# Seven block products in three PSUM banks, six such pairs a layer, in an encoder kernel on one core

## The chip, the core and the metric

The kernel runs on one core of a Trainium2 chip. TensorE (PE) multiplies matrices into PSUM, eight banks of 512 float32 columns for each of the 128 partitions; VectorE (DVE), ScalarE (ACT) and GpSimd (POOL) work on SBUF and PSUM; SyncE (SP) issues transfers. Each engine runs its own instructions in the order in which the program gives them, and waits on semaphores for the others. The metric is the device time of one execution in microseconds.

## The reference

Two layers over x of 512 positions and 1024 channels, in float32. Cut to what matters here:

```python
h = rmsnorm(x, norm1[l])
p = h @ w_in[l]                                # Fourier group | q | k | v
y_f = fourier_mix(u, w_fourier[l], b_fourier[l])
y_a = windowed_gqa(q, k, v, sink[l])
mix = concat([rmsnorm(y_f, ...), rmsnorm(y_a, ...)])
x = x + mix @ w_o[l]
h = rmsnorm(x, norm2[l])
up = dwconv_centred(h @ w_up[l], conv_w[l], conv_b[l])
gate, val = up[..., :D_FF], up[..., D_FF:]     # D_FF = 2816
x = x + (silu(gate) * val) @ w_down[l]
```

The convolution has width 3 along the positions. The change lies in the last four lines, the ConvFFN.

## The kernel before

Channels lie on partitions, positions along the free dimension, so `x` is eight tiles of 128x512. A float32 product is made of three matmuls of rounded parts (`mm3`: high by high on L121, low by high on L122, high by low on L123). A weight tile is split by `wsplit` into `whi` (ACT, L91) and `wlo` (DVE, L94: the raw tile less its high part); there are five buffers of each. Raw weights (`wraw`, three buffers) come by SP (L130).

The FFN of a layer goes over 22 pairs `fi` of channel blocks (gate and value), in groups of 8, 7 and 7 pairs; after each group its part of `w_down` is multiplied, eight output blocks of 8 or 7 blocks deep. A pair is made in one of two ways:

- `up_eight`: for gate and value each, two splits and 24 matmuls of 512 columns into one bank, then one DVE multiplication by `rb2` (the reciprocal norm, by position) out of PSUM.
- `up_seven`: gate and value are taken together as a 2 by 2 block product, over two halves of the input channels and two halves of the positions (`LO` and `HI`, 256 columns), with seven block products in place of eight (the Winograd form). That is 84 matmuls of 256 columns. The weights of four of the products are the sums s1 to s4 that DVE makes in `tA` tiles; seven tiles are split. X, Y and Z are sums in PSUM: X holds B11, then T2 is added, then T3 or T4; Y holds T1, then B22 is added; Z holds B21. Between the steps ACT copies X and Y out (`act(ua..)`, `act(ub..)`) and DVE adds. Before, X and Y are the two halves of one bank and Z is in a second.

The seven products of the activations need sums of the normed blocks too (T1 to T4); `sums_of_h` makes them once a layer: ACT loads eight blocks, DVE makes 16 subtractions or additions of 256 columns and eight low parts of 512, into `m4` tiles and the `room` tiles. T1 and T3 lie in one tile, T2 and T4 in another.

Then follow for each pair the convolution (`conv`: ACT once, DVE twice on L97, for gate and for value), silu on ACT, a product on DVE and its split into `slab` or `pT`.

Beside this, layer 0 splits part of layer 1's weights ahead (`presplit`): one job per pair or per `w_down` block loads a tile (`praw`, by SP), splits it into two `tA` tiles on ACT and DVE, and stores both to DRAM (`kept`), 88 stores in all, on SP's queue one job late (`late`, `store`). Layer 1 fetches them.

`rb2` comes from a sum of squares: transposing matmuls, DVE makes `nv` (L208), POOL raises it to the power -1/2 (`nr`, L210), PE broadcasts it (L233), ACT copies it out (`rb`). The order of the instructions on each engine comes from the framework's scheduler, which simulates the engines over the program; the program's own order is what it starts from. PSUM banks are taken in turn from the list `FFN_BANKS`, whose names stand for pools of three (`mm`), two (`sc`, `tp`) and one (`av`) banks. There are six `tF`, six `tA` and two `praw` buffers.

Of the kernel before, what the change touches and what calls it, by code (L numbers as in the profile page):

```python
# [12 lines left out]
ALU = mybir.AluOpType  # L13
# [15 lines left out]
FT = DFF // P  # L29
# [1 line left out]
NEG = -1.0e30  # L31
NWARM = 10
RATE, STEP0 = 1, 12
FFN_BANKS = ("mm", "mm", "mm", "av", "sc", "sc")
GROUPS = [(0, 8), (8, 7), (15, 7)]
SEVEN = [range(2, FT, 3), range(2, FT, 3)]


def encoder_kernel(tc, t):
# [7 lines left out]
    nc = tc.nc  # L47
# [9 lines left out]
    tp = pool(name="temps", bufs=2)  # L57
# [11 lines left out]
    def f(x):  # L69
        return x.bitcast(F32)  # L70
# [19 lines left out]
    def act(out, in_, func=AF.Copy, **kw):  # L90
        return nc.scalar.activation(out, in_, func, **kw)  # L91

    def tt(out, a, b, op, eng=None):
        return (eng or nc.vector).tensor_tensor(out, a, b, op=op)  # L94
# [41 lines left out]
    def wsplit(raw, eng=None, hi_eng=None):  # L136
        hi = wp.tile([P, 512], F32R, tag="whi", name=nm("whi"), bufs=5)
        lo = wp.tile([P, 512], F32R, tag="wlo", name=nm("wlo"), bufs=5)
        n = raw.shape[-1]
        if hi_eng is None:  # L140
            pace[0] = act(hi[:, :n], raw).ins
        else:
            hi_eng.tensor_copy(hi[:, :n], raw)
        tt(lo[:, :n], raw, f(hi)[:, :n], ALU.subtract, eng)
        return hi, lo
# [5 lines left out]
    kept = {}  # L151

    def presplit(l):

        late = []

        def keep(key, src):
            n = src.shape[-1]
            two = [temp(n, "tA", F32R) for _ in range(2)]
            with tc.issue_after(pace[0]):  # L160
                act(two[0], src)
            tt(two[1], src, f(two[0]), ALU.subtract)
            kept[key] = [dp.tile([P, n], F32, tag=f"{key}{s}", name=nm("kept")) for s in range(2)]
            store()
            late.append(lambda: [nc.sync.dma_start(o, f(z)) for o, z in zip(kept[key], two)])

        def store():
            while late:
                late.pop()()

        def load(src):
            raw = temp(512, "praw")[:, :src.shape[-1]]
            nc.sync.dma_start(raw, src)
            return raw

        jobs = []
        for grp in (1, 0):
            for k in range(KT):
                c = (k % 2) * 384
                jobs.append((f"qkv{grp}{k}", lambda g=grp, k=k, c=c: load(t["w_qkv"][l, g, k // 2, :, c:c + 384])))  # L180
        for k in range(KT):
            jobs.append((f"u{k}", lambda k=k: load(t["w_in"][l, k * P:(k + 1) * P, 0:FW])))
        for j in range(NF):
            jobs.append((f"f{j}", lambda j=j: load_wf(l, j, temp(512, "praw"))))
        for half in range(2):
            for m in range(KT):
                jobs.append((f"o{half}{m}", lambda h=half, m=m: load(t["w_o"][l, h, :, m * 512:(m + 1) * 512])))
        got = jobs[0][1]()
        for n, (key, _) in enumerate(jobs):
            raw = got  # L190
            if n + 1 < len(jobs):
                got = jobs[n + 1][1]()
            keep(key, fold_wu(raw) if key[0] == "u" else fold_wf(raw) if key[0] == "f" else raw)
            yield
        store()
        while True:
            yield

# [181 lines left out]
    LO, HI = slice(0, 256), slice(256, 512)  # L380

    def bank():
        nps[0] += 1
        return psum(FFN_BANKS[nps[0] % len(FFN_BANKS)])

# [9 lines left out]
    def sums_of_h(l, h2):  # L395

        room = rooms()
        out = []
        for k in range(4):
            b = [temp(512, "tF") for _ in range(2)]  # L400
            for i in range(2):
                act(b[i], x[k + 4 * i], scale=g2[:, l, k + 4 * i:k + 4 * i + 1])
            t13, t24 = temp(512, "tF"), temp(512, "tF")
            tt(t13[:, LO], b[0][:, HI], b[0][:, LO], ALU.subtract)
            tt(t13[:, HI], b[1][:, HI], b[0][:, HI], ALU.subtract)
            tt(t24[:, LO], t13[:, LO], b[1][:, HI], ALU.subtract)
            tt(t24[:, HI], t24[:, LO], b[1][:, LO], ALU.add)
            r13, r24 = [next(room), next(room)], [next(room), next(room)]
            split(*r13, t13)
            split(*r24, t24)  # L410
            out.append(dict(B11=[z[:, LO] for z in halves(h2[k])], B21=[z[:, LO] for z in halves(h2[k + 4])],
                            B22=[z[:, HI] for z in halves(h2[k + 4])], T1=[z[:, LO] for z in r13],
                            T3=[z[:, HI] for z in r13], T2=[z[:, LO] for z in r24], T4=[z[:, HI] for z in r24]))
        return out
# [14 lines left out]
    def up_seven(l, fi, h2, ts, rb2):  # L429
        a, b = [wload(t["w_up"][l, fi + z * FT], 1024) for z in range(2)]  # L430
        a11, a12, a21, a22 = a[:, :512], a[:, 512:], b[:, :512], b[:, 512:]
        xy, zz = bank(), bank()
        X, Y, Z = xy[:, LO], xy[:, HI], zz[:, LO]
        ua, ub = temp(512, "tF"), temp(512, "tF")

        def product(o, w, key, start=False):
            for k in range(4):
                mm3(o, [z[:, k * P:(k + 1) * P] for z in w], ts[k][key], start and k == 0, k == 3, skip_group_check=True)

        product(X, wsplit(a11), "B11", True)  # L440
        act(ua[:, LO], X)
        s1, s2, s3, s4 = [temp(512, "tA") for _ in range(4)]
        tt(s1, a21, a22, ALU.add)
        product(Y, wsplit(s1), "T1")
        act(ub[:, HI], Y)
        tt(s3, a11, a21, ALU.subtract)
        tt(s2, s3, a22, ALU.subtract)
        product(X, wsplit(s2), "T2")
        act(ua[:, HI], X)
        product(Z, wsplit(a12), "B21", True)  # L450
        tt(ua[:, LO], ua[:, LO], Z, ALU.add)
        product(X, wsplit(s3), "T3")
        tt(ub[:, HI], ub[:, HI], X, ALU.add)
        tt(s4, a12, s2, ALU.add)
        product(Y, wsplit(s4), "B22")
        tt(ua[:, HI], ua[:, HI], Y, ALU.add)
        tt(ua, ua, rb2, ALU.mult)
        yield ua
        product(X, wsplit(a22), "T4")
        tt(ub[:, LO], X, rb2[:, LO], ALU.mult)  # L460
        tt(ub[:, HI], ub[:, HI], rb2[:, HI], ALU.mult)
        yield ub
# [11 lines left out]
    for l in range(L):  # L474
# [4 lines left out]
        for grp in (1, 0):  # L479
# [14 lines left out]
            z = temp(1536, "pT").rearrange("p (b c) -> p b c", b=NB)  # L494
# [303 lines left out]
        if l == 0:  # L798
            tabs, alts, wt = load_tables(1)
        ahead = presplit(l + 1) if l < L - 1 else iter(lambda: 0, 1)  # L800
        ts = sums_of_h(l, h2)
        for f0, nf in GROUPS:
            gu = []
            for fi in range(f0, f0 + nf):
                n = fi - f0
                ys_ = [conv(l, fi + z * FT, u) for z, u in enumerate((up_seven if fi in SEVEN[l] else up_eight)(l, fi, h2, ts, rb2))]
                next(ahead)
                act(ys_[0], ys_[0], AF.Silu)
                tt(ys_[0], ys_[0], ys_[1], ALU.mult)
                if n < 4:  # L810
                    a = pair("slab")
                else:
                    if n % 2 == 0:
                        two = temp(2048, "pT", F32R).rearrange("p (n s q) -> p n s q", n=2, s=2)
                    a = two[:, n % 2]
                split(a[:, 0, :], a[:, 1, :], ys_[0])
                gu.append(a)
            nxt = []
            for m in range(KT):
                next(ahead)  # L820
                w = wchunks(t["w_down"][l, m, :, f0 * P:(f0 + nf) * P], nf * P)
                end = l == L - 1 and f0 + nf == FT
                nh = 2 if end and m == KT - 1 else 1
                for h in range(nh):
                    q0, q1 = h * S // nh, (h + 1) * S // nh
                    o = bank()[:, q0:q1]
                    for k in range(nf):
                        mm3(o, [z[:, (k % 4) * P:(k % 4 + 1) * P] for z in w[k // 4]],
                            [gu[k][:, s, q0:q1] for s in range(2)], k == 0, k == nf - 1)
                    tt(x[m][:, q0:q1], x[m][:, q0:q1], o, ALU.add)  # L830
                    if end:
                        nc.sync.dma_start(t["out"][m, :, q0:q1], x[m][:, q0:q1])
                if l < L - 1 and f0 + nf == FT:
                    nxt.append(norm_tile(m, g1[:, l + 1, :], acc))
            xg = nxt
# [88 lines left out]
```

## Time and profile before

| | |
|---|---|
| median of 2 runs | 1152.34 us (1151.12 to 1153.57) |
| profiled execution | 1152.17 us, span 1150.4 us, mean granted TensorE clock 0.966 |
| PE busy | 1064.2 us, 93% of the span |
| DVE busy | 813.5 us, 71% |
| ACT busy | 549.2 us, 48% |
| POOL busy | 65.3 us, 6% |
| FFN of layer 0 | about 201 to 581 us of the span |
| FFN of layer 1 | about 763 to 1150 us of the span |

A row of the profile names the line, the engine, the operation and its tiles without their numbers (`tF<-ps` reads PSUM and writes a tF tile). Times are microseconds from the span's start. In brackets stands the time that the engine was idle before, and what ended it. Matmuls are pipelined, so their cost is read from start to start, not from the length of one. Instructions of a helper carry the helper's line: L91 is every ACT operation, L94 every two-input DVE operation, so they are told apart by their tiles.

### The profile page before, as it was taken

How to read it: one execution, taken by the hardware profiler on the slowest of the kernel's cores; microseconds unless marked ns; L12 is line 12 of the kernel's file. 1: busy time of each engine (PE TensorE's matmuls, PEld its weight loads, DVE VectorE, ACT ScalarE, POOL GpSimd, SP SyncE). 2: the span in 40 equal slices, each digit the busy share in tenths (PEclk: the TensorE clock that was granted, in tenths of full speed). 3: DMA queues.
4: the chain of work that ended last, by engine and by line, in shares of the span. 5: the costliest groups of instructions: out<-in, count | busy, mean ns of one | idle time of the engine just before them, and what ended most of it. 6: DMA issues, size and time to landing. Idle time of an engine off the chain costs nothing.

```text
span 1150.4 us, 15741 instructions
## 1 busy us (share of the span) xinstructions
PE 1064.2 (93%) x5599; PEld 910.9 (79%) x5599; DVE 813.5 (71%) x1624; ACT 549.2 (48%) x1055; POOL 65.3 (6%) x142
## 2 busy tenths in 40 slices
PE   8998899789997989997999989996899989999898
PEld 7976688678886878787879967885788878778787
DVE  7967669786758778667676866496865487647863
ACT  5259637554434444344443595264543354324541
POOL 0005200000000000000010052020000000000000
PEclk9999999899999989988999999998999999999999
DMA  8220032334843438544677402521233222232233
GB/s 274 75 91 20 19 98 87 114 102 151 246 155 126 153 111 280 173 135 140 191 237 222 164 19 76 182 74 57 91 100 102 92 75 87 80 123 79 88 85 101
DMA packets 60547, 140.13 MB, mean 122 GB/s; under 512 B 6706, under 2 KB 20274, under 8 KB 60468
## 3 DMA queue, kind: packets, MB, share of 16 engines
q1 hardware_dynamic: 60468, 139.12, 38.1%
q8 instruction: 44, 0.72, 0.2%
q14 instruction: 35, 0.29, 0.1%
HBM read 116.02 MB, written 23.07 MB: 121 GB/s over the span
## 4 chain that ended last, share of the span: by engine, by line
PE 66%; DVE 18%; issue 8%; ACT 4%; DMA 3%; POOLq 1%; POOL 0%; SPq 0%; DVEq 0%; ACTq 0%
PE ps L121 20%; PE ps L122 20%; PE ps L123 19%; DVE tF L97 5%; DVE tF L94 3%; DVE tA L94 3%; PE ps L119 3%; DVE wlo L94 3%; DMA wraw<-in_w_up_dram 1%; PE ps L644 1%; ACT tA L91 1%; PE ps L625 1%; PE ps L637 1%; DVE tA L629 1%; DMA wraw<-in_w_qkv_dram 1%
## 5 line engine op out<-in xcount | busy, mean ns | idle before, releaser
L91 ACT ACTIVATE whi<-wraw 128x512 fp32r<-128x512 f32 (+1 forms) x282 | 169.5, 613 | 291.8 <-PE ps L123 256.5
L122 PE MATMUL ps<-act,wlo 128*128 128x512 f32 (+1 forms) x712 | 262.1, 369 | 0.4 <-DVE wlo L94 0.4
L94 DVE TENSOR_TENSOR wlo<-wraw,whi 128x512 fp32r<-128x512 f32 (+1 forms) x290 | 189.5, 664 | 102.5 <-ACT whi L91 100.4
L121 PE MATMUL ps<-act,whi 128*128 128x512 f32 (+1 forms) x712 | 260.9, 369 | 0.0
L123 PE MATMUL ps<-act,whi 128*128 128x512 f32 (+1 forms) x712 | 260.9, 368 | 0.0
L122 PEld LDWEIGHTS ps<-act,wlo 128*128 128x128 f32 x712 | 136.9, 192 | 22.5 <-DVE wlo L94 1.0
L121 PEld LDWEIGHTS ps<-act,whi 128*128 128x128 f32 x712 | 137.1, 192 | 21.4
L123 PEld LDWEIGHTS ps<-act,whi 128*128 128x128 f32 x712 | 136.8, 192 | 21.1
L97 DVE SCALAR_TENSOR_TENSOR tF<-tF,pb,tF 128x511 f32<-128x511 f32 x176 | 127.7, 743 | 4.4 <-ACT tF L91 3.6
L121 PE MATMUL ps<-slab,whi 128*128 128x512 f32 (+2 forms) x276 | 105.7, 386 | 3.1 <-ACT slab L91 2.6
L122 PE MATMUL ps<-slab,wlo 128*128 128x512 f32 (+2 forms) x276 | 105.6, 383 | 1.8 <-DVE wlo L94 1.8
L123 PE MATMUL ps<-slab,whi 128*128 128x512 f32 (+2 forms) x276 | 105.3, 384 | 1.1 <-DVE slab L94 1.1
L91 ACT ACTIVATE tF<-tF,pb 128x512 f32<-128x512 f32 x88 | 71.3, 811 | 44.9 <-DVE tF L94 23.5
L121 PE MATMUL ps<-m,whi 128*128 128x256 f32 x140 | 46.2, 330 | 47.2 <-ACT whi L91 25.3
L94 DVE TENSOR_TENSOR tF<-ps,rb 128x512 f32<-128x512 f32 (+1 forms) x90 | 57.0, 642 | 36.3 <-PE ps L123 31.8
L94 DVE TENSOR_TENSOR x<-x,ps 128x512 f32<-128x512 f32 (+1 forms) x65 | 42.6, 675 | 56.4 <-PE ps L123 56.4
L121 PEld LDWEIGHTS ps<-m,whi 128*128 128x128 f32 x140 | 31.0, 222 | 52.5 <-ACT whi L91 26.6
L121 PEld LDWEIGHTS ps<-slab,whi 128*128 128x128 f32 x276 | 52.1, 189 | 14.6 <-ACT slab L91 3.5
L122 PE MATMUL ps<-pT,wlo 128*128 128x512 f32 (+1 forms) x163 | 62.9, 387 | 0.5 <-DVE wlo L94 0.5
L121 PE MATMUL ps<-pT,whi 128*128 128x512 f32 (+1 forms) x163 | 62.9, 387 | 0.1
L122 PEld LDWEIGHTS ps<-slab,wlo 128*128 128x128 f32 x276 | 52.2, 189 | 11.9 <-DVE wlo L94 2.1
L123 PEld LDWEIGHTS ps<-slab,whi 128*128 128x128 f32 x276 | 52.1, 189 | 11.8 <-DVE slab L94 1.9
(192 smaller groups left out, 1897.1 us busy)
## 6 DMA issues: line engine op xcount, KB each, us to landing
wraw<-in_w_up_dram SPq DMA_DIRECT2D x88, 512.0 KB, 3.6
kept<-tA SPq DMA_DIRECT2D x56, 256.0 KB, 3.4
wraw<-in_w_down_dram SPq DMA_DIRECT2D x32, 448.0 KB, 3.4
wraw<-in_w_down_dram SPq DMA_DIRECT2D x16, 512.0 KB, 3.7
whi<-kept SPq DMA_DIRECT2D x28, 256.0 KB, 3.5
wlo<-kept SPq DMA_DIRECT2D x28, 256.0 KB, 3.7
kept<-tA SPq DMA_DIRECT2D x32, 192.0 KB, 2.8
wraw<-in_w_o_dram SPq DMA_DIRECT2D x8, 512.0 KB, 3.7
```

The lines of the kernel that those rows point to most:

```text
L91: return nc.scalar.activation(out, in_, func, **kw)
L94: return (eng or nc.vector).tensor_tensor(out, a, b, op=op)
L97: return nc.vector.scalar_tensor_tensor(out=out, in0=a, scalar=s, in1=b, op0=op0, op1=op1)
L119: nc.tensor.matmul(out, a[0], b[0], start=start, stop=stop, **kw)
L121: nc.tensor.matmul(out, a[0], b[0], start=start, stop=False, **kw)
L122: nc.tensor.matmul(out, a[1], b[0], start=False, stop=False, **kw)
L123: nc.tensor.matmul(out, a[0], b[1], start=False, stop=stop, **kw)
L625: nc.tensor.matmul(sc[:, :n], qT[p][:, e, i * P:(i + 1) * P], kT[g][:, s, j0 * P:(j1 + 1) * P], start=s == 0, stop=s == 1)
L629: nc.vector.tensor_tensor_reduce(out=pr[:, :n], in0=sc[:, :n], in1=mask[:, m0:m0 + n], scale=qs_scale[p][:, i, e:e + 1], scalar=nsink[:, l ...
L637: tr = nc.tensor.transpose(pp[:, j * P:(j + 1) * P], pr[:, j * P:(j + 1) * P], ident)
L644: pv = nc.tensor.matmul(py[64 * e:64 * e + 64, i0 * P:(i1 + 1) * P], vp[:, j, 64 * g:64 * g + 64], pT[:, half, e, b0:b0 + 2 * (i1 - i0) + ...
```

## The change

Five edits, all in the FFN:

- `SEVEN` begins with pair 5 in place of pair 2: pairs 5, 8, 11, 14, 17, 20 of each layer are seven pairs, and pair 2 is an eight pair.
- X, Y and Z of a seven pair get a bank each, and the products alternate between them: B11 (X), T1 (Y), B21 (Z), T2 (X), B22 (Y), T3 (X), T4 (X). Before, the program has B11, T1, T2, B21, T3, B22, T4.
- `FFN_BANKS` has the two `tp` banks as well, eight in all.
- `sums_of_h` is called after the first pair of the layer and its `presplit` job, not ahead of the loop.
- The stores of `presplit` are issued by GpSimd's queue at once, not by SP's one job later.

```diff
-FFN_BANKS = ("mm", "mm", "mm", "av", "sc", "sc")
+FFN_BANKS = ("mm", "mm", "mm", "av", "sc", "sc", "tp", "tp")
-SEVEN = [range(2, FT, 3), range(2, FT, 3)]
+SEVEN = [range(5, FT, 3), range(5, FT, 3)]
...
             kept[key] = [dp.tile([P, n], F32, tag=f"{key}{s}", name=nm("kept")) for s in range(2)]
-            store()
-            late.append(lambda: [nc.sync.dma_start(o, f(z)) for o, z in zip(kept[key], two)])
-
-        def store():
-            while late:
-                late.pop()()
+            for o, z in zip(kept[key], two):
+                nc.gpsimd.dma_start(o, f(z))
...
-        xy, zz = bank(), bank()
-        X, Y, Z = xy[:, LO], xy[:, HI], zz[:, LO]
+        X, Y, Z = [bank()[:, LO] for _ in range(3)]
...
         tt(s1, a21, a22, ALU.add)
-        product(Y, wsplit(s1), "T1")
+        product(Y, wsplit(s1), "T1", True)
         act(ub[:, HI], Y)
+        product(Z, wsplit(a12), "B21", True)
+        tt(ua[:, LO], ua[:, LO], Z, ALU.add)
         tt(s3, a11, a21, ALU.subtract)
         tt(s2, s3, a22, ALU.subtract)
         product(X, wsplit(s2), "T2")
         act(ua[:, HI], X)
-        product(Z, wsplit(a12), "B21", True)
-        tt(ua[:, LO], ua[:, LO], Z, ALU.add)
+        tt(s4, a12, s2, ALU.add)
+        product(Y, wsplit(s4), "B22")
         product(X, wsplit(s3), "T3")
         tt(ub[:, HI], ub[:, HI], X, ALU.add)
-        tt(s4, a12, s2, ALU.add)
-        product(Y, wsplit(s4), "B22")
...
-        ts = sums_of_h(l, h2)
+        ts = None
...
                 next(ahead)
+                if ts is None:
+                    ts = sums_of_h(l, h2)
```

The order in which the scheduler then puts the instructions, at three places. ACT in layer 1, around the first copy out of X in pair 11, before: `ps_1978` is the bank of X and Y, `whi_1994`, `whi_1996` and `whi_1999` are the pair's last three split weights, `slab` and the `tF` rows with `pb` are the pairs ahead of it.

```order
L91 ACTIVATE whi_1994_9154<-tA_1986_9098 128x512
L91 ACTIVATE tF_1966_9021<-tF_1965_9019,pb_96 128x512
L91 ACTIVATE whi_1996_9172<-tA_1987_9099 128x512
L91 ACTIVATE whi_1999_9194<-wraw_1977_9073 128x512
L91 ACTIVATE tF_1974_9062<-tF_1973_9060,pb_96 128x512
L91 ACTIVATE slab_1958_8981<-tF_1949_8934 128x512
L91 ACTIVATE tF_1980_9077<-ps_1978_9075 128x256
L91 ACTIVATE tF_1966_9021<-tF_1966_9021 128x512
L91 ACTIVATE tF_1981_9078<-ps_1978_9075 128x256
```

And now, with X in `ps_1966` and Y in `ps_1967`; `whi_1983`, `whi_1985` and `whi_1988` are the last three weights.

```order
L91 ACTIVATE whi_1983_9038<-tA_1976_8982 128x512
L91 ACTIVATE whi_1985_9054<-tA_1975_8981 128x512
L91 ACTIVATE slab_1946_8863<-tF_1937_8816 128x512
L91 ACTIVATE tF_1962_8944<-tF_1961_8942,pb_96 128x512
L91 ACTIVATE tF_1969_8960<-ps_1966_8957 128x256
L91 ACTIVATE whi_1988_9077<-wraw_1965_8955 128x512
L91 ACTIVATE tF_1954_8903<-tF_1954_8903 128x512
L91 ACTIVATE tF_1970_8961<-ps_1967_8958 128x256
```

The pair's last weight moved from ahead of X's copy to behind it, and the two copies read two banks.

DVE in layer 0, from `nv` to the first multiplications by `rb2` (`rb_418`), before: the 128x256 rows and the rows into `m4` and `room` belong to `sums_of_h`.

```order
L208 TENSOR_SCALAR nv_415_1884<-ps_414_1879 128x4
L94 TENSOR_TENSOR wlo_492_2135<-wraw_488_2128,whi_491_2134 128x512
L94 TENSOR_TENSOR tF_446_1961<-tF_445_1960,tF_444_1957 128x256
L94 TENSOR_TENSOR m4_442_1951<-tF_440_1945,m4_442_1951 128x512
L94 TENSOR_TENSOR wlo_509_2193<-wraw_502_2184,whi_508_2192 128x512
L94 TENSOR_TENSOR tF_446_1961<-tF_446_1961,tF_444_1957 128x256
```

And now, the same place; `wlo_504` to `wlo_514` are weights of pair 2, an eight pair.

```order
L201 TENSOR_SCALAR nv_415_1884<-ps_414_1879 128x4
L94 TENSOR_TENSOR wlo_504_2189<-wraw_502_2186,whi_503_2188 128x512
L94 TENSOR_TENSOR wlo_506_2193<-wraw_502_2186,whi_505_2192 128x512
L94 TENSOR_TENSOR wlo_512_2230<-wraw_510_2227,whi_511_2229 128x512
L94 TENSOR_TENSOR tF_437_1959<-ps_436_1934,rb_418_1893 128x512
L94 TENSOR_TENSOR wlo_514_2234<-wraw_510_2227,whi_513_2233 128x512
L94 TENSOR_TENSOR tF_445_2000<-ps_444_1975,rb_418_1893 128x512
```

The sums that stood ahead of `rb2`'s first use now follow it, among the convolutions of the first pairs.

SP at the end of layer 0's FFN, before: loads for `presplit` (`praw`) and stores (`kept`) in turn.

```order
L173 DMA praw_1221_5417<-in_w_o_dram 128x512
L165 DMA kept_1212_5375<-tA_1210_5371 128x512
L165 DMA kept_1224_5423<-tA_1222_5419 128x512
L173 DMA praw_1234_5466<-in_w_o_dram 128x512
L165 DMA kept_1225_5424<-tA_1223_5420 128x512
L130 DMA wraw_1280_5652<-in_w_down_dram 128x896
```

And now; the stores stand on POOL's queue.

```order
L130 DMA wraw_1260_5517<-in_w_down_dram 128x896
L167 DMA praw_1192_5266<-in_w_o_dram 128x512
L167 DMA praw_1204_5313<-in_w_o_dram 128x512
L130 DMA wraw_1268_5556<-in_w_down_dram 128x896
L167 DMA praw_1217_5362<-in_w_o_dram 128x512
```

SP's queue holds loads alone in this stretch.

More of the change, by code (lines that the diff above doesn't have):

```diff
@@ L153, in presplit @@
     def presplit(l):
-        late = []
         def keep(key, src):
@@ L194, in presplit @@
             yield
-        store()
         while True:
```

## The prediction

> **What bounds the kernel now.** I read the page's busy times and its chain first, then both FFN stretches side by side, then what TensorE waited for ahead of the seven products, then the single waits.
>
> ```profile
> PE 1064.2 (93%) x5599; PEld 910.9 (79%) x5599; DVE 813.5 (71%) x1624; ACT 549.2 (48%) x1055; POOL 65.3 (6%) x142
> PE 66%; DVE 18%; issue 8%; ACT 4%; DMA 3%; POOLq 1%; POOL 0%; SPq 0%; DVEq 0%; ACTq 0%
> ```
>
> TensorE (PE) is busy 93% of the span and holds two thirds of the chain. So the time can fall in two ways only: fewer matmul columns, or fewer gaps and half-clock matmuls. The stretch view (us; busy PE, PEld, DVE, ACT, POOL; granted clock; DMA share; GB/s) gives the FFN of layer 0, then that of layer 1:
>
> ```profile
> 201.00:555.00 354.00, 316.41 (x1601) 272.62 (x1600) 256.69 (x444) 160.73 (x277) 0.00 (x0) 0.94 0.49 155
> 768.00:1151.00 383.00, 355.03 (x1817) 303.80 (x1815) 257.34 (x423) 163.29 (x272) 8.28 (x1) 0.97 0.28 88
> ```
>
> PE is without work for 354.00 - 316.41 = 37.6 us in the first and 383.00 - 355.03 = 28.0 us in the second, at clocks of 0.94 and 0.97. Most of that stands ahead of the T products of the seven-product pairs. The tile view of `m` (the tiles m4 that hold most T sums) names for each window what ended PE's idle time, in us and number of times; the first three lines are layer 0, the last is layer 1:
>
> ```profile
>   ACT whi L91: 25.3, 6
>   DVE wlo L94: 11.1, 6
>   ACT tF L91: 0.5, 1
> ```
>
> ```profile
>   ACT tF L91: 21.4, 12
> ```
>
> The causes differ. In layer 0 T1 waits for its weights: s1 is made late on VectorE (DVE), so its high part (and behind it the low part) comes late. In layer 1 the weights are there, and T1 and T2 wait for ScalarE (ACT) to evict X, with which Y shares a bank. PE's timeline around single waits, with the idle time and its releaser in brackets:
>
> ```profile
> 212.66 0.58 PE L121 MATMUL ps<-m,whi 128*128 128x256 f32 x1 [6.67 <-ACT whi L91]
> 252.48 0.38 PE L121 MATMUL ps<-m,whi 128*128 128x256 f32 x1 [3.38 <-ACT whi L91]
> 370.79 0.58 PE L121 MATMUL ps<-m,whi 128*128 128x256 f32 x1 [5.26 <-ACT whi L91]
> 410.30 0.41 PE L121 MATMUL ps<-m,whi 128*128 128x256 f32 x1 [3.37 <-ACT whi L91]
> 488.57 0.38 PE L121 MATMUL ps<-m,whi 128*128 128x256 f32 x1 [2.85 <-ACT whi L91]
> 528.61 0.39 PE L121 MATMUL ps<-m,whi 128*128 128x256 f32 x1 [3.79 <-ACT whi L91]
> 778.49 0.38 PE L233 MATMUL ps<-ident,nr 128*128 128x128 f32 x1 [2.48 <-POOL nr L210]
> 793.13 0.58 PE L121 MATMUL ps<-m,whi 128*128 128x256 f32 x1 [7.18 <-ACT tF L91]
> 830.01 0.39 PE L121 MATMUL ps<-m,whi 128*128 128x256 f32 x1 [2.73 <-ACT tF L91]
> ...
> 830.54 0.41 PE L121 MATMUL ps<-m,whi 128*128 128x256 f32 x1
> ...
> 832.25 0.41 PE L123 MATMUL ps<-room,whi 128*128 128x256 f32 x1
> ```
>
> These are pairs 2, 5, 11, 14, 17 and 20 of layer 0, then rb2 and pairs 2 and 5 of layer 1. The matmuls behind a wait run slower: from 830.54 to 832.25 are eight starts, 0.214 us each.
>
> **PE's own work.** At full clock, three spacings of 512 columns lie between the first two rows, three of 256 between the last two:
>
> ```profile
> 203.72 0.39 PE L121 MATMUL ps<-act,whi 128*128 128x512 f32 x1
> ...
> 204.40 0.28 PE L121 MATMUL ps<-act,whi 128*128 128x256 f32 x1
> ...
> 204.75 0.28 PE L121 MATMUL ps<-act,whi 128*128 128x256 f32 x1
> ```
>
> 0.68 / 3 = 0.227 and 0.35 / 3 = 0.117. An eight pair is 48 x 0.227 = 10.9 us, a seven pair 84 x 0.117 = 9.8 to 10.0. Pair 2 of each layer becomes an eight: +0.9 us per layer, on the path wherever PE sets the end (in layer 1 in full).
>
> **Layer 1, the banks.** With X, Y, Z apart, T1 (in Y) needs no eviction, and its weights are early: in the new order DVE makes s1 of pair 5 ahead of the evictions of pairs 2 to 4. What comes next is T2, which goes into X and stands 24 matmuls (T1 and B21, 2 x 1.4 = 2.8 us) behind B11, where before only B21 lay between. How long ACT takes to that eviction is seen in pair 5:
>
> ```profile
> 827.37 0.63 ACT L91 ACTIVATE whi<-wraw 128x512 fp32r<-128x512 f32 x1 [0.70 <-ACT whi L91]
> 827.90 0.80 ACT L91 ACTIVATE tF<-tF,pb 128x512 f32<-128x512 f32 x1
> 829.06 0.63 ACT L91 ACTIVATE slab<-tF 128x512 fp32r<-128x512 f32 x1 [0.35 <-DVE tF L94]
> 829.59 0.37 ACT L91 ACTIVATE tF<-ps 128x256 f32<-128x256 f32 x1
> ```
>
> B21 ended at 830.01 - 2.73 = 827.28, and only then could this weight tile be overwritten; convolution, slab and eviction follow, ending 2.7 us later. In the new order of pairs 11, 14, 17 and 20 ACT's last weight split ahead of the eviction takes B11's buffer, so the same row of work starts at B11's end and is done some 2.7 us later, against T2's 2.8. That just fits; I keep 0.6 us of wait for each of five pairs. In pair 5 a split for the next pair (waiting for B21's buffer) stands ahead of the eviction, and PE has that pair's first 12 matmuls between: I keep 1.3 us (a split of 0.63 and as much again from engine to engine, as in the 0.70 before 827.37). So 21.4 - 5 x 0.6 - 1.3 = 17.1 us go. Both ends: 21.4 if nothing waits, and 21.4 - 6 x 2.73 = 5.0 if every pair waits as pair 5 does now (pair 2's own wait goes in any case, since it is no longer a seven). I take 17.1, as the rows of ACT name the work exactly.
>
> The half-clock matmuls behind those waits: about 13 a pair x (0.214 - 0.117) = 1.2 us, five long waits, 6 us; with waits under 1.3 us I let 5 go. The Trainium skill, "TensorE: Matmul & The Clock Gate", Part 1, has the clock fall after an idle window of about 3.4 us; the row at 830.54 shows slow matmuls after 2.73 us already, which that free-running window does not forbid. By the rule alone only pair 2's wait would have cost clock for certain, and the term would be 1.2 instead of 5.
>
> **Layer 1, sums_of_h later.** Its 16 half-wide and 8 full subtractions stood on DVE while POOL took the power for rb2:
>
> ```profile
> 194.99 1.39 POOL L210 TENSOR_TENSOR nr<-nv,mhalf 128x4 f32<-128x4 f32 x1 [47.31 <-DVE nv L208]
> 770.15 8.28 POOL L210 TENSOR_TENSOR nr<-nv,mhalf 128x4 f32<-128x4 f32 x1 [49.87 <-DVE nv L208]
> ```
>
> Now weight subtractions that wait for buffers follow nv, and the sums come behind rb2's first evictions. I take the power at 1.4 us, the other row, so PE's 2.48 us at 778.49 go. The Trainium skill, "SBUF — State Buffer", Who interferes with whom, says that a DVE instruction with two SBUF inputs and a GpSimd one that reads SBUF lock each other out whole; the 8.28 agrees, the 1.39 beside equally dense DVE work does not. Layer 1: -17.1 - 5 - 2.5 + 0.9 = -23.7 us.
>
> **Layer 0.** There DVE is the late one, and the sums move into its full stretch. The same stretch view for the sums' place now, and from rb2 to the wait of pair 5; below it DVE's first eviction and s1 of pair 5:
>
> ```profile
> 188.00:202.50 14.50, 14.50 (x73) 12.28 (x72) 12.85 (x29) 11.19 (x20) 1.39 (x1) 1.00 0.14 40
> 202.50:252.30 49.80, 38.09 (x201) 33.05 (x200) 39.91 (x67) 26.66 (x46) 0.00 (x0) 0.90 0.36 115
> ```
>
> ```profile
> 202.70 1.89 DVE L94 TENSOR_TENSOR tF<-ps,rb 128x512 f32<-128x512 f32 x3 [1.38 <-ACT rb L91]
> ...
> 251.09 0.68 DVE L94 TENSOR_TENSOR tA<-wraw 128x512 f32<-128x512 f32 x1
> ```
>
> In the new order 75 DVE instructions stand from the first eviction to s1 of pair 5 (sums included, pair 2's s and T work gone). At 39.91 / 67 = 0.596 us each that is 44.7 us: s1 starts at 202.70 + 44.7 = 247.4, and with s1 and its split on ACT (0.6 each) T1 starts at about 248.6, say 248, for 252.48 now. PE meanwhile has pairs 2, 3 and 4 as eights and B11: 204.40 + 3 x 10.9 + 1.4 = 238.5, so it waits some 9.5 us there, longer than any wait now; yet the place in the program is reached 4.5 us earlier (pair 2's extra 0.9 us of matmuls lies inside that wait, and so costs nothing in this layer). Ends: if the 16 half-wide ones take half, 41 us and 8 us earlier; if DVE waits as in this stretch (49.80 - 39.91 = 9.9 us), 5 us later than now.
>
> Behind it, T1 of pairs 11, 14 and 20 keeps waiting for s1, behind the last evictions and convolutions. Pair 17's order is unchanged at 2.85 us; I let the others come down to that: (5.26 - 2.85) + (3.37 - 2.85) + (3.79 - 2.85) = 3.9 us, and pair 8's 0.5 us for X's eviction goes.
>
> **The stores of the split weights.** 88 stores leave SP's queue, where they wait and hold what follows:
>
> ```profile
> kept<-tA SPq DMA_DIRECT2D x56, 256.0 KB, 3.4
> kept<-tA SPq DMA_DIRECT2D x32, 192.0 KB, 2.8
> 574.02 0.63 ACT L91 ACTIVATE tA<-praw 128x512 fp32r<-128x512 f32 x1 [3.83 <-issue]
> ```
>
> At 574.02 ACT waits 3.83 us for a block behind such stores, at the end of the layer; PE's weight work is queued behind it. I take 1 us of gain (0 to 3.8). On POOL no row shows a store. From below: its small operations take 1.0 to 1.4 us; from above: 8.28. POOL has nothing else in this layer's 354 us, so stores hide there up to 354 / 88 = 4.0 us each; I take the 1.39, measured beside dense DVE work, and cost nothing. The Trainium skill, "DMA: Bandwidth & Descriptors", gives a DMA from GpSimd about 2.0 us plus its bytes; by it, as an estimate 2.6 us for 256 KB, nothing changes in the sum. Layer 0: -4.5 - 3.9 - 0.5 - 1 = -9.9; I round to -9.
>
> **Sum.** 1152.2 (the profiled execution; span 1150.4, and the median of the runs is 1152.34) - 23.7 - 9 = 1119.5 us.
>
> **Rivals.** *DVE takes it back.* Layer 0 gains nothing (s1 of pair 5 later, the gain lost in the later pairs), and ACT keeps half of layer 1's 17 us: 1152 - (8.5 + 5 + 2.5 - 0.9) = 1137. For it: DVE's 39.91 busy of 49.80 and waits between; against it: fewer seven pairs, each with more DVE work than an eight. *Better.* DVE comes level in layer 0 because T4, B22 and the evictions have banks of their own; of the 37 us ahead of the T products there another 15 go: 1105. *Slower: POOL becomes the queue that is late.* If a store holds POOL for over 4.0 us, stores pile up, tA tiles (six) stay taken, and s1 to s4, which need four of them, wait. At 4.5 us: 88 x 0.5 = 44 us of layer 0, none of its 9 gained, layer 1's 23.7 kept: 1172. For it: 8.28 us; against it: 1.39 beside the same work. [...] *It does nothing:* T1 still ordered behind X's eviction by something else than the bank; then only pair 2's 7.2 and rb2's 2.5 us go, less 0.9: 1143.
>
> **Chances.** Forecast 0.58 (1108 to 1129), better 0.10, DVE takes it back 0.18, slower 0.09, nothing 0.05. About 2% (23 us; below 1129 or above 1175) is what I count as a change that a measurement tells. Faster 0.66 (the first two, less 0.02 for the forecast's upper edge); within 2% 0.26 (the second and the last rival, part of POOL's); slower 0.08. The range leaves out the far end of the better case and POOL's: 1100 to 1146.
>
> **What would show it.** In layer 1 the tile view of `m` should name ACT tF with under 6 us instead of 21.4, and the clock should be 0.98 or more; pair 5 should have the longest wait. In layer 0 PE should wait 8 to 11 us ahead of T1 of pair 5, at about 248, released by ACT's split. POOL's power for rb2 should take under 2 us. POOL's rows for stores, or waits of DVE or ACT for tA released by POOL's queue, decide the slower rival. The forecast is wrong if layer 0's stretch gets longer than now, or if T2 in layer 1 waits as long as T1 does now.

## The result and the profile after

The changed kernel takes 1100.39 us (median of 2 runs, 1099.13 to 1101.65) for 1152.34 before: a ratio of 0.9549, 95% interval 0.9485 to 0.9613. The forecast was 1119.5 in a range from 1100 to 1146, so the direction was right, but the gain, 52 us, is 1.6 times the 32.7 that the sum gave, and the time lies at the very edge of the range: 0.4 us from its lower end, with one of the two runs below it. The profiled execution took 1099.13 us, its span is 1097.3 us.

The page of the changed kernel, busy times and chain:

```profile
PE 1049.7 (96%) x5527; PEld 897.8 (82%) x5527; DVE 798.5 (73%) x1602; ACT 543.2 (50%) x1043; POOL 108.5 (10%) x230
PE 82%; DVE 9%; ACT 3%; DMA 3%; issue 2%; POOL 0%; SPq 0%; ACTq 0%; DVEq 0%; POOLq 0%
```

DVE's part of the chain is halved, PE's is up from 66% to 82%. To place the gain I cut both spans at the last matmul of `w_o` and of `w_down` in each layer. The stretch view with these cuts (start and end; length; busy PE, PEld, DVE, ACT, POOL; granted clock; DMA share; GB/s), first of the kernel before, from the span's start to its end:

```profile
0.00:157.80 157.80, 145.24 (x797) 122.55 (x798) 113.82 (x330) 86.67 (x211) 27.61 (x73) 0.98 0.30 97
157.80:597.30 439.50, 399.82 (x1966) 340.92 (x1966) 328.71 (x570) 210.69 (x363) 4.92 (x7) 0.95 0.50 158
597.30:732.00 134.70, 128.13 (x860) 113.65 (x859) 84.73 (x253) 70.39 (x180) 24.52 (x61) 1.00 0.42 129
732.00:1150.40 418.40, 391.03 (x1979) 333.73 (x1978) 286.19 (x471) 181.44 (x301) 8.28 (x1) 0.97 0.29 90
```

and of the changed kernel:

```profile
0.00:154.20 154.20, 142.19 (x797) 120.62 (x798) 113.62 (x330) 86.43 (x211) 27.49 (x73) 1.00 0.31 100
154.20:573.80 419.60, 395.51 (x1922) 335.80 (x1922) 322.58 (x559) 210.02 (x357) 55.19 (x95) 0.96 0.52 166
573.80:711.60 137.80, 131.26 (x869) 116.00 (x868) 84.79 (x253) 70.39 (x180) 24.38 (x61) 0.99 0.41 127
711.60:1097.30 385.70, 380.74 (x1943) 325.34 (x1942) 277.49 (x460) 176.37 (x295) 1.42 (x1) 1.00 0.32 98
```

Layer 0's FFN is 19.9 us shorter, layer 1's 32.7; the two stretches that the change doesn't touch cancel (-3.6 and +3.1). PE's idle time falls from 39.7 to 24.1 us in layer 0 and from 27.4 to 5.0 in layer 1, where the granted clock is 1.00. The tile view of `m`, in the changed kernel: layer 0 (200 to 575 us), then layer 1:

```profile
  ACT whi L91: 18.0, 5
  DVE wlo L94: 4.5, 5
```

```profile
  ACT tF L91: 0.2, 1
```

In layer 1 the 21.4 us of waiting for X's eviction are 0.2. In layer 0 five seven pairs still wait for s1. PE's timeline around pairs 5 and 11 of layer 0, and pair 5 of layer 1:

```profile
241.65 0.58 PE L121 MATMUL ps<-m,whi 128*128 128x256 f32 x1 [6.62 <-ACT whi L91]
244.06 0.58 PE L122 MATMUL ps<-m,wlo 128*128 128x256 f32 x1 [1.31 <-DVE wlo L94]
355.67 0.39 PE L121 MATMUL ps<-m,whi 128*128 128x256 f32 x1 [2.85 <-ACT whi L91]
357.47 0.58 PE L122 MATMUL ps<-m,wlo 128*128 128x256 f32 x1 [0.90 <-DVE wlo L94]
796.02 0.50 PE L121 MATMUL ps<-act,whi 128*128 128x512 f32 x1 [0.72 <-ACT whi L91]
797.49 0.49 PE L122 MATMUL ps<-act,wlo 128*128 128x512 f32 x1 [0.97 <-DVE wlo L94]
```

And ACT in pair 11 of layer 1, around the eviction of X (the `tF<-ps` row), with PE's first T1 matmul, the next after B11's last, and its first T2 matmul ahead of them:

```profile
902.39 0.28 PE L121 MATMUL ps<-m,whi 128*128 128x256 f32 x1
...
905.27 0.28 PE L121 MATMUL ps<-m,whi 128*128 128x256 f32 x1
```

```profile
902.59 0.63 ACT L91 ACTIVATE whi<-tA 128x512 fp32r<-128x512 f32 x1 [0.80 <-PE ps L123]
903.12 0.62 ACT L91 ACTIVATE slab<-tF 128x512 fp32r<-128x512 f32 x1
903.65 0.80 ACT L91 ACTIVATE tF<-tF,pb 128x512 f32<-128x512 f32 x1
904.35 0.36 ACT L91 ACTIVATE tF<-ps 128x256 f32<-128x256 f32 x1
```

Row by row this is what the prediction walked through: the split that takes B11's buffer, slab, convolution, eviction, done at 904.71, that is 2.3 us after B11's end, while T2 starts 2.9 us after it. T1 and B21 cover it, and T2 doesn't wait.

### The profile page after: what moved, and what is told of

Its sections match the earlier page's. It is cut to its first block, busy times and chain, and to the rows that moved or that the text cites. A ratio compares the mean times of both kernels' runs of the same rounds, so it can differ in the third digit from the quotient of the medians.

```text
span 1097.3 us, 15620 instructions
## 1 busy us (share of the span) xinstructions
PE 1049.7 (96%) x5527; PEld 897.8 (82%) x5527; DVE 798.5 (73%) x1602; ACT 543.2 (50%) x1043; POOL 108.5 (10%) x230
## 4 chain that ended last, share of the span: by engine, by line
PE 82%; DVE 9%; ACT 3%; DMA 3%; issue 2%; POOL 0%; SPq 0%; ACTq 0%; DVEq 0%; POOLq 0%
PE ps L122 25%; PE ps L123 25%; PE ps L121 24%; PE ps L119 3%; DVE tF L97 2%; DVE tA L94 2%; DMA wraw<-in_w_qkv_dram 1%; DMA praw<-in_w_o_dram 1%; PE ps L636 1%; ACT tA L91 1%; DVE tF L94 1%; DVE wlo L94 1%; PE ps L629 1%; PE ps L617 1%; DVE tA L621 1%
## 5 line engine op out<-in xcount | busy, mean ns | idle before, releaser
L91 ACT ACTIVATE whi<-wraw 128x512 fp32r<-128x512 f32 (+1 forms) x284 | 171.9, 613 | 251.9 <-PE ps L123 218.5
L121 PE MATMUL ps<-act,whi 128*128 128x512 f32 (+1 forms) x720 | 268.0, 373 | 1.0 <-ACT whi L91 0.7
L122 PE MATMUL ps<-act,wlo 128*128 128x512 f32 (+1 forms) x720 | 267.0, 371 | 1.0 <-DVE wlo L94 1.0
L123 PE MATMUL ps<-act,whi 128*128 128x512 f32 (+1 forms) x720 | 265.7, 371 | 0.0
L94 DVE TENSOR_TENSOR wlo<-wraw,whi 128x512 fp32r<-128x512 f32 (+1 forms) x292 | 192.1, 664 | 97.8 <-ACT whi L91 95.7
L163 POOL DMA_DIRECT2D kept<-tA x88 | 47.7, 543 | 320.7 <-ACT tA L91 270.9
L121 PE MATMUL ps<-pT,whi 128*128 128x512 f32 (+1 forms) x163 | 62.7, 386 | 0.0
L123 PE MATMUL ps<-pT,whi 128*128 128x512 f32 (+1 forms) x163 | 60.7, 385 | 0.0
```

The costliest lines, as they stand in the source:

```text
L121: nc.tensor.matmul(out, a[0], b[0], start=start, stop=False, **kw)
L122: nc.tensor.matmul(out, a[1], b[0], start=False, stop=False, **kw)
L123: nc.tensor.matmul(out, a[0], b[1], start=False, stop=stop, **kw)
L163: nc.gpsimd.dma_start(o, f(z))
```

## The experiments

The stages below are cut as above, each from one profile of that kernel; the medians come from several runs beside the kernel before on the same chip, where that took 1149.9 to 1151.5 us. Behind each time stands the range of its runs; the ratio is to the kernel before, with its 95% interval. A stage difference of 3 us or less says little: the first stage, whose instructions are the same in every kernel, took 154.0 to 158.9 us over the profiles.

**One part undone at a time.** The shared bank first:

```diff
-        X, Y, Z = [bank()[:, LO] for _ in range(3)]
+        xy, zz = bank(), bank()
+        X, Y, Z = xy[:, LO], xy[:, HI], zz[:, LO]
...
-        product(Y, wsplit(s1), "T1", True)
+        product(Y, wsplit(s1), "T1")
```

> The changed kernel, but X and Y are again the two halves of one bank. If the shared bank was what TensorE waited for in layer 1, the waits ahead of T products of layer 1, released by ACT tF, come back: now 0.2 us, then 10 to 20 us, with 3 to 8 us of half clock behind them, 1113 to 1128 us in all, and layer 0 as in the changed kernel. If instead the new product order or pair 2 made the gain of layer 1, they stay under 3 us and the time under 1104.

It took 1112.01 us (1109.35 to 1113.0), ratio 0.9674 (0.9653 to 0.9696), 12 us over the changed kernel. The tile view, layer 1:

```profile
  ACT tF L91: 6.1, 9
```

Layer 1's FFN is 398.1 us for 385.7, layer 0's 419.0 for 419.6. So the bank is worth 12 us, all in layer 1. That is under half of layer 1's gain, and the waits are far from the 21.4 of before. The separate bank is not the whole of the mechanism.

The sums ahead of the loop again:

```diff
-        ts = None
+        ts = sums_of_h(l, h2)
...
-                if ts is None:
-                    ts = sums_of_h(l, h2)
```

> The changed kernel, but sums_of_h ahead of the loop as before. In layer 1, if dense sums beside it made POOL's power for rb2 8.28 us long, that comes back with TensorE's 2.5 us wait: +2 to +5 us. In layer 0 the sums lie in DVE's free 12 us ahead of rb2 again, so T1 of pair 5 no longer waits 6.6 us: -4 to -8. Together 1094 to 1102 us. If the later sums were a gain in both layers, over 1106.

It took 1090.98 us (1087.86 to 1092.3), ratio 0.9488 (0.9461 to 0.9515): some 9 us faster than the changed kernel, and under the range of the prediction. Stretch view of its two FFNs, and PE at T1 of pair 5 in layer 0:

```profile
157.80:570.60 412.80, 392.27 (x1921) 333.22 (x1920) 322.66 (x559) 210.40 (x357) 55.48 (x95) 0.98 0.52 168
706.90:1089.80 382.90, 379.72 (x1943) 325.40 (x1941) 278.55 (x460) 177.87 (x295) 1.39 (x1) 1.00 0.32 98
```

```profile
241.32 0.39 PE L121 MATMUL ps<-m,whi 128*128 128x256 f32 x1 [2.72 <-ACT whi L91]
```

Layer 0 is 6.8 us shorter, and the wait of pair 5 falls from 6.62 to 2.72, to the level of the other pairs. Putting the sums later was a loss: ahead of rb2 DVE has little else to do. The stretch view of the changed kernel for the 14.50 us up to DVE's first multiplication by rb2, with 4.56 us of DVE work; the kernel before had 12.85 in the same place:

```profile
183.90:198.40 14.50, 14.50 (x73) 12.25 (x73) 4.56 (x8) 3.82 (x8) 1.42 (x1) 1.00 0.27 83
```

Behind rb2 the same work lies ahead of s1. POOL's power in layer 1 takes 1.39 us here with the sums ahead of rb2, and 1.42 in the changed kernel with them behind it.

Pair 2 as a seven pair again:

```diff
-SEVEN = [range(5, FT, 3), range(5, FT, 3)]
+SEVEN = [range(2, FT, 3), range(2, FT, 3)]
```

> The changed kernel, but with pair 2 of each layer a seven pair again. Theory: in layer 0 s1 of pair 2 and the sums come late on DVE, so T1 waits 6 us or more and pair 5 still 3 us; in layer 1 the sums are due behind rb2, about 10 us of DVE work, and T1 of pair 2 waits some us: 1106 to 1118. Rival: with three banks pair 2 costs nothing and its 0.9 us of matmuls a layer are a gain: 1097 to 1100.

It took 1120.83 us (1119.91 to 1123.55), ratio 0.9758 (0.9737 to 0.9780), more than expected. Pair 2 of layer 0:

```profile
223.23 0.58 PE L121 MATMUL ps<-m,whi 128*128 128x256 f32 x1 [17.66 <-ACT whi L91]
```

With the sums late, pair 2 must wait 17.7 us for s1. So pair 2 as an eight pair is worth some 20 us beside the late sums. It doesn't make them harmless: by the run above they cost some 9 us even so.

The stores on SP's queue again:

```diff
+        late = []
...
-            for o, z in zip(kept[key], two):
-                nc.gpsimd.dma_start(o, f(z))
+            store()
+            late.append(lambda: [nc.sync.dma_start(o, f(z)) for o, z in zip(kept[key], two)])
+
+        def store():
+            while late:
+                late.pop()()
...
+        store()
```

> The changed kernel, but the 88 stores on SP's queue, one job late, as before. Theory: only the end of layer 0 is longer, by the 2.8 us that the changed kernel gained in its last w_down: 1101 to 1105. Rival: the stores on SP held the loads of W_up or tA tiles all through layer 0, and much of layer 0's 20 us of gain is theirs: over 1108.

It took 1101.46 us (1098.61 to 1103.41), ratio 0.9584 (0.9560 to 0.9608); layer 0's FFN took 418.8 us. The stores' queue made no difference that shows. On POOL they cost nothing either; the group of the 88 stores in the changed kernel, and POOL's waits behind it:

```profile
L163 POOL DMA_DIRECT2D kept<-tA x88 | 47.7, 543 | 320.7 <-ACT tA L91 270.9
```

They took 0.54 us each, and POOL waited 320.7 us for their data: it was never the late queue.

Six banks instead of eight:

```diff
-FFN_BANKS = ("mm", "mm", "mm", "av", "sc", "sc", "tp", "tp")
+FFN_BANKS = ("mm", "mm", "mm", "av", "sc", "sc")
```

> The changed kernel, but with six banks in the FFN's turn instead of eight. If the two added banks carry part of the gain (TensorE would else wait for evictions while DVE is late in layer 0 and behind rb2 in layer 1), new waits of PE for DVE's eviction rows, 1106 to 1118 us. If they were only spare room, 1098 to 1104 us.

It took 1101.15 us (1099.86 to 1102.36), ratio 0.9561 (0.9547 to 0.9575). The two added banks are spare room only.

**One part alone.** The kernel before with the new `up_seven` and eight banks:

> The kernel before with one part of the change alone: three banks for X, Y and Z, the new product order, eight banks; pair 2 stays a seven pair, the sums ahead of the loop, the stores on SP. Bank theory: the ACT tF waits of layer 1 (21.4 us) fall under 4 and their half clock goes, pair 2 included unless its sums are late; layer 0 keeps its waits for s1: 1120 to 1130. Rival: pair 2 and the sums carried layer 1: 1138 to 1150.

It took 1108.37 us (1107.33 to 1110.01), ratio 0.9625 (0.9611 to 0.9639): 43 us of the gain, faster than either theory had it. Against the run with the sums first, which differs in pair 2 and in the store queue, it shows that pair 2 as an eight pair is worth 17 us with the sums early too. Its two FFNs:

```profile
156.00:578.80 422.80, 394.84 (x1958) 336.57 (x1957) 328.03 (x570) 213.09 (x363) 5.22 (x7) 0.96 0.52 164
715.10:1106.40 391.30, 381.00 (x1979) 328.07 (x1977) 282.94 (x471) 180.36 (x301) 5.47 (x1) 0.99 0.32 96
```

This part alone takes 16.7 us off layer 0 too, where the shared bank had made almost no wait. So the order of the products had to be told from the bank: the kernel before with the order alone, X and Y in one bank.

```diff
         product(Y, wsplit(s1), "T1")
         act(ub[:, HI], Y)
+        product(Z, wsplit(a12), "B21", True)
+        tt(ua[:, LO], ua[:, LO], Z, ALU.add)
...
         act(ua[:, HI], X)
-        product(Z, wsplit(a12), "B21", True)
-        tt(ua[:, LO], ua[:, LO], Z, ALU.add)
+        tt(s4, a12, s2, ALU.add)
+        product(Y, wsplit(s4), "B22")
         product(X, wsplit(s3), "T3")
         tt(ub[:, HI], ub[:, HI], X, ALU.add)
-        tt(s4, a12, s2, ALU.add)
-        product(Y, wsplit(s4), "B22")
```

> The kernel before with the new product order alone: X and Y still halves of one bank, six banks, pair 2 a seven pair, sums ahead of the loop. The run with the banks, the order and eight banks alone gave 1108. If the separate bank made the gain of both layers: 1140 to 1152, layer 0's FFN 435 to 440 us, layer 1's over 400. If the order alone relieves layer 0 (T1 followed by B21, which needs nothing, so that the wait for the low part of s1 is shorter and half clock less): layer 0's FFN 420 to 428, layer 1's 395 to 410, 1118 to 1135.

It took 1126.9 us (1123.93 to 1127.12), ratio 0.9787 (0.9766 to 0.9808). Stretch view of its FFNs, and the tile view of layer 0 and then of layer 1:

```profile
156.00:581.90 425.90, 396.88 (x1957) 338.11 (x1956) 328.78 (x570) 212.91 (x363) 4.54 (x7) 0.96 0.51 163
720.20:1125.20 405.00, 385.96 (x1979) 329.35 (x1977) 286.08 (x471) 181.04 (x301) 8.28 (x1) 0.99 0.30 93
```

```profile
  ACT whi L91: 20.8, 6
  DVE wlo L94: 5.4, 6
```

```profile
  ACT tF L91: 12.9, 11
```

And ACT in pair 11 of layer 1, with the T1 matmul that waits for it:

```profile
924.38 0.64 ACT L91 ACTIVATE whi<-tA 128x512 fp32r<-128x512 f32 x1 [0.86 <-PE ps L123]
...
926.14 0.36 ACT L91 ACTIVATE tF<-ps 128x256 f32<-128x256 f32 x1
```

```profile
926.56 0.39 PE L121 MATMUL ps<-m,whi 128*128 128x256 f32 x1 [0.84 <-ACT tF L91]
```

The eviction's row of work starts at B11's end now, 1.4 us (B21) earlier against PE than before, and 0.84 us is left of T1's wait. The order alone shortens the FFNs by 13.6 and 13.4 us, with the bank still shared; the bank then takes another 3.1 and 13.7. So in layer 1 about half of what the two do together belongs to the order, and in layer 0 most of it. The separate banks with the old order were not run.

**No seven pairs.** In layer 0 a seven pair saves 0.9 us of matmuls and mostly waits 4 to 8 us (2.85 and 0.70 to 0.90 in four of the six, 6.62 and 1.31 in pair 5, nothing in pair 8). So without them there:

```diff
-SEVEN = [range(5, FT, 3), range(5, FT, 3)]
+SEVEN = [range(0), range(5, FT, 3)]
...
-                if ts is None:
+                if ts is None and SEVEN[l]:
```

> The changed kernel with no seven pairs in layer 0 (and no sums there); layer 1 unchanged. Theory: in layer 0 the 22.5 us ahead of T products and the half clock behind them (about 8 us) go, and six pairs cost 0.9 us more matmuls each: 1100 - 30.5 + 5.5 = 1075 (1068 to 1083). Rival: DVE is the bound of layer 0 whatever the pairs, and other waits take the place: over 1092.

It took 1067.04 us (1065.09 to 1073.1), ratio 0.9274 (0.9244 to 0.9303): 33 us faster than the changed kernel.

```profile
157.20:540.80 383.60, 383.60 (x1706) 318.01 (x1705) 283.36 (x465) 188.47 (x305) 54.41 (x95) 1.00 0.56 180
677.40:1063.30 385.90, 380.92 (x1943) 325.27 (x1942) 278.44 (x460) 178.00 (x295) 1.01 (x1) 1.00 0.32 98
```

Layer 0's FFN is 36.0 us shorter than the changed kernel's; PE has no idle time and the granted clock is 1.00. So DVE is not the bound of layer 0 whatever the pairs. But without the seven pairs it also has 39 us less work (283.36 for 322.58), and the run doesn't part that from the wait for s1.

With the sums first in layer 1 beside it:

> As the kernel without seven pairs in layer 0, and in layer 1 the sums ahead of the loop. Theory from the run with the sums first: layer 1's first group takes 2.8 us less (154.4 for 157.2), as the wait of 1.9 us for pair 6's weights in pair 5 goes: 1072, 2 to 3 us under the run without seven pairs in layer 0. Rival: POOL's power for rb2 is held up by the sums (8.28 us in the kernel before), and it is 1 to 3 us over it.

It took 1067.72 us (1064.52 to 1071.38), ratio 0.9281 (0.9256 to 0.9307): no difference. The 2.8 us by which layer 1 seemed shorter with the sums first is not borne out.

On this last kernel, none in layer 1 either (`SEVEN = [range(0), range(0)]`), and then nine in layer 1 (`range(4, FT, 2)`):

> No seven pairs in either layer, so no sums; the rest as in the run without them in layer 0 and with the sums first (1067.7). Theory: in layer 1 the seven pairs wait for nothing and save their 0.9 us of matmuls each, so without them 6 x 0.9 = 5.5 us more: 1071 to 1075. Rival: the sums and half-wide products cost layer 1 as much as they save: 1063 to 1068.

> As the run without seven pairs in layer 0 and with the sums first (1067.7), but in layer 1 every second pair from 4 to 20 a seven pair, nine instead of six. Theory: three more save 3 x 0.9 = 2.8 us: 1063 to 1066. Rival: DVE, with some 10 us of work a pair for 10.4 us of TensorE's, gets late, and waits ahead of T1 come back: over 1070.

They took 1067.81 us (1066.59 to 1074.05), ratio 0.9292 (0.9267 to 0.9318), and 1067.7 us (1064.9 to 1075.63), ratio 0.9300 (0.9269 to 0.9331). None, six or nine seven pairs in layer 1 can't be told apart. In the profiles layer 1's FFN is 385.9 us with six of them, against 390.2 with none here and 387.3 with none in the last kernel below: 1 to 4 us, under the 5.5 that the matmuls alone would give and hardly more than such stages scatter.

Last, the kernel before with no seven pairs, its banks and stores as they were:

> The kernel before with no seven pairs in either layer (and no sums); six banks and the stores on SP as they were. If the seven pairs' waits are all that parts the two kernels and more, it comes to the changed kernel without seven pairs (1067.8): 1066 to 1072, so that banks, order and stores are worth nothing without seven pairs. Rival: the eight banks or POOL's stores carry some gain of their own: over 1078.

It took 1067.34 us (1063.02 to 1068.3), ratio 0.9289 (0.9262 to 0.9317), with the granted clock at 1.000 over the profiled span. Without seven pairs nothing is left for the rest of the change to do. Its whole gain is a part of the price that the seven pairs had: in the kernel before the 14 of them saved 0.9 us of matmuls each, 13 us over both layers, and cost some 83 us more than that (1149.92 us beside it on the same chip, less 1067.34).

## Why the prediction was right or wrong

**The path.** The stages add up from single-part kernels (us; differences of the stretch views, one profile each; the store queue and the two banks are left out since neither showed where they were undone):

| step | FFN layer 0 | FFN layer 1 |
|---|---|---|
| before | 439.5 | 418.4 |
| product order alone | 425.9 | 405.0 |
| and a bank each | 422.8 | 391.3 |
| and pair 2 an eight pair | 412.8 | 382.9 |
| and the sums late (the changed kernel) | 419.6 | 385.7 |

The sum had layer 1 at -23.7 and layer 0 at -9; they came to -32.7 and -19.9. The range holds the time by luck: 1100.39 lies outside the 1108 to 1129 that had most of the chance, and it lies above 1100 only because one edit that was counted as a gain, the late sums, cost some 9 us. Without it the change took 1090.98.

**Layer 1, the T waits: right in place and size, half right in cause.** 17.1 us were forecast, 21.4 - 0.2 - (0.72 + 0.97) = 19.5 came, with the new wait at pair 5 where it was put (1.3 forecast, 1.7 measured). What failed is the step "with X, Y, Z apart, T1 needs no eviction" as the cause of it all: the order alone brought these waits from 21.4 to 12.9, of which 7.5 are pair 2's; with the order, pair 2 an eight pair and the bank still shared, 6.1 were left, and only these are the separate bank's. With the new order X's eviction is no longer queued on ACT behind a split that waits for B21; the prediction had seen that row on ACT, but counted it as part of the bank's effect.

**The half-clock matmuls: mis-sized.** 5 us were forecast. The stage fell by 32.7; 19.5 of waits and 2.5 at rb2, less 0.9 of matmuls, leave 32.7 - 21.1 = 11.6 us. Counted from start to start over the stage (what lies over 0.227 us for 512 columns and 0.12 for 256, idle time taken out), slow matmuls cost some 12 us before and 2 now, so about 10. The 1.2 us a pair stopped at the next wait. In three of the five pairs with a long wait the starts stay slow behind that too, and the five lost some 1.6 to 2.1 us each. The sum also left out what follows rb2's wait of 2.48 us, seven slow starts worth 1.6. PE in the kernel before, behind the wait of 7.18 us of pair 2, behind that of pair 11, and behind rb2's:

```profile
793.51 0.41 PE L122 MATMUL ps<-m,wlo 128*128 128x256 f32 x1
...
795.64 0.41 PE L123 MATMUL ps<-room,whi 128*128 128x256 f32 x1
```

```profile
943.13 0.58 PE L121 MATMUL ps<-m,whi 128*128 128x256 f32 x1 [2.78 <-ACT tF L91]
943.51 0.41 PE L122 MATMUL ps<-m,wlo 128*128 128x256 f32 x1
...
945.64 0.41 PE L123 MATMUL ps<-room,whi 128*128 128x256 f32 x1
```

```profile
780.20 0.63 PE L123 MATMUL ps<-act,whi 128*128 128x512 f32 x1
780.63 0.63 PE L121 MATMUL ps<-act,whi 128*128 128x512 f32 x1
```

Ten spacings take 2.13 us behind 7.18 us of waiting and behind 2.78 alike. By the rule that the prediction took from the Trainium skill, "TensorE: Matmul & The Clock Gate", Part 1 (the clock falls after an idle window of about 3.4 us), the term was 1.2 us, with pair 2's wait alone sure to cost clock; the trace goes against that even more than against the 5.

**The sums behind rb2: wrong.** The step "the sums come behind rb2's first evictions", taken at -2.5 us in layer 1 and as part of a net gain in layer 0, is a loss of about 7 us in layer 0. rb2's wait did go, but the late sums were not needed for it. POOL's power for rb2 in layer 1 of the kernel with the order alone, of the one with the banks as well, of the one with the sums first but pair 2 an eight pair, and of the one with the sums late but pair 2 a seven pair:

```profile
758.22 8.28 POOL L210 TENSOR_TENSOR nr<-nv,mhalf 128x4 f32<-128x4 f32 x1 [49.81 <-DVE nv L208]
```

```profile
751.65 5.47 POOL L210 TENSOR_TENSOR nr<-nv,mhalf 128x4 f32<-128x4 f32 x1 [48.30 <-DVE nv L208]
```

```profile
744.06 1.39 POOL L203 TENSOR_TENSOR nr<-nv,mhalf 128x4 f32<-128x4 f32 x1 [48.90 <-DVE nv L201]
```

```profile
763.05 1.38 POOL L203 TENSOR_TENSOR nr<-nv,mhalf 128x4 f32<-128x4 f32 x1 [47.03 <-DVE nv L201]
```

It is long where pair 2 is a seven pair and the sums stand first, and short if either is changed. Sums beside it do not suffice to make it long.

**Layer 0: mis-sized, the other way.** T1 of pair 5 came at 241.65, for a forecast of 248. Of this, 3.6 us lie ahead of the FFN, in the first stage, whose instructions are the same. DVE, from its first multiplication by rb2 to s1 of pair 5:

```profile
198.42 0.69 DVE L94 TENSOR_TENSOR tF<-ps,rb 128x512 f32<-128x512 f32 x1 [2.38 <-ACT rb L91]
...
240.25 0.69 DVE L94 TENSOR_TENSOR tA<-wraw 128x512 f32<-128x512 f32 x1
```

The 75 instructions took 41.8 us, near the lower end (41), not the 44.7 taken: the mean came from the old stretch, with only five half-wide ones in it, and the new row has sixteen. PE waited 6.62 us, not 9.5, and the place was gained by 7.2 us, counted from the end of `w_o`, not 4.5. The floor of 2.85 us for pairs 11, 14, 17 and 20 held to the hundredth. But the sum left out the waits for the low part, which went from 11.1 to 4.5 us over the layer, and some 3 us of slow matmuls (counted as above). That is most of the 19.9 - 9 = 11 us by which this layer beat the sum. It is the order that took most of the low part's waits, and the sum gave it nothing here: with the order alone they are 5.4 us already. In pair 5 of that kernel DVE comes to the low part of s1 one row sooner, 2.47 us after s1 (248.75 to 251.22) for 3.07 before (251.09 to 254.16).

**The stores: nothing.** 1 us was forecast, none shows. The bound of 4.0 us for which a store could hold POOL was never near: 0.54, so the slower rival is out. From issue to landing a store took 3.9 us from POOL's queue (3.4 and 2.8 from SP's before), where the prediction's estimate was 2.6.

**The rivals.** "DVE takes it back" and "it does nothing" are out by the time alone. "Better" (1105) is nearest, but not for its reason: DVE did not come level, T1 still waits 2.85 us in four later pairs, and what took time from layer 0 was the order (13.6 us) and pair 2 (10.0), hardly the banks (3.1). The rival that was missing is the one that the runs brought out: that a seven pair in this kernel costs more than it saves, so that the largest gain of the change lay in making fewer or cheaper seven pairs.

## What to carry to other kernels

A trick that saves matmuls has to be priced with the waits it makes: compare it on the chip with the plain form before its waits are tuned away. Here 0.9 us of matmuls a pair had been bought in layer 0 with mostly 4 to 8 us of TensorE waiting for sums made by a busy VectorE, and dropping it there beat every arrangement of it that was run. In layer 1 dropping it made no difference that could be told. When two edits go at the same wait (an order and a bank), run each alone, since either may bring most of the gain.

## What the runs showed of the hardware

Waits cost more than their length: layer 1's 22 us of idle time that went had 10 to 12 us of slow matmuls behind them, nearly all of it behind waits of 2.48 to 7.18 us, and the longest wait lost no more than those of 2.7. Behind waits of 0.84 us, in the kernel with the order alone, the starts were 0.12 us apart again after one.

The same operation on POOL, which reads and writes SBUF alone in the rows of these traces, took 1.0 to 8.28 us. Where it was long, it ended 0.86 to 0.87 us after a row of two-input DVE instructions had stopped: at 757.12 after 756.25 in the run with 5.47, at 778.43 after 777.56 in the kernel before, and at 766.50 after 765.64 with the order alone. The Trainium skill, "SBUF — State Buffer", Who interferes with whom, has such a lock, and the long cases agree with it. The 1.39 us beside an equally dense row in the kernel with the sums first does not, and what decides between them stays open.

Equal instructions ahead of the FFN took from 154.0 to 158.9 us from one profile to the next.
